# A hybrid decoder layer on one core: x and two of its input blocks first, memory keys and values after the S5 branch

## The chip, the cores and the metric

The kernel runs on one core of one Trainium2 chip. The metric is the device time of one execution in microseconds (us), the median of several runs; a profile of one further execution shows where its time goes.

## The reference, cut to what matters

One step of one layer, for a prompt of 512 tokens and 8 single sample tokens that share the weights (520 columns in all):

```python
h = rmsnorm(x, norm1_g)
u, q, k, v, qm, gl = split(h @ w_in)          # 512 | 768 | 768 | 768 | 512 | 3 x 1024 columns
A = glu(gelu(S5(u)))                          # 32 groups, 64 complex states each, scan over tokens
B = dilated_window_attention(q, k, v) @ w_att_o
C = cross_attention(qm, rmsnorm(mem, mem_norm_g) @ w_mem_kv) @ w_mem_o   # 256 memory tokens; samples: cached k, v
x = x + (sum_b sigmoid(gl_b) * branch_b) @ w_out
a, v2 = split(rmsnorm(x, norm2_g) @ w_up)
x = x + (gelu(causal_conv3(a)) * v2) @ w_down
y = rmsnorm(x, final_norm_g)
```

D_MODEL is 1024, D_FF 2816. The states, keys, values and memory keys and values are outputs too.

## The kernel before, in words

**Products.** Activations lie with features on the 128 partitions, in eight blocks of 520 columns. Every fp32 product is three products of high and low parts: the weight tile (128x1024, 512 KB) is fetched by `wload` (L160, on the SP queue), rounded to its high part by ScalarE (L163, `wh`), and VectorE takes the rest (L80, `wl`). One call of `dense` makes one block of 128 output features: for each of eight k blocks, in two halves of 260 columns, wh by xh (L192), wh by xl (L193) and wl by xh (L195), 48 matmuls in all. L80 is the line of the helper `tt`, so all tensor-by-tensor work of VectorE and GpSimd bears it. There are two PSUM tiles for dense blocks, two buffers for raw weights and four for high and low parts; `wahead(AHEAD)` keeps four tiles on their way.

**Order.** A framework sets the order of each engine's queue from the program order, priorities (`urgent`) and its own cost estimates; each engine then runs its queue strictly in that order and waits on semaphores. On top of it a class `Side` runs generators beside the dense blocks: after every k block `side.pe(...)` advances a clock by the block's cost, and a generator whose time has come may issue its next piece, so that small matmuls of S5, attention and samples stand between dense ones.

**Stages.** The stages stand in this order: memory statistics and keys (`ps_mk`, L494 to L498), memory values (`ps_mv`, L519 to L521), and the four S5 input blocks u0 to u3; memory queries qm0 to qm3, k0 to k5 and q0 to q5 with S5 beside them; v0 to v5 with memory attention (`mem_prompt`) beside them; `ssm_gated(0)` to `(5)` (a gate block `ps_g` and the GLU pair `ps_ga`, `ps_gb`: 96 matmuls each) with windowed attention (`att_prompt`) beside them; then `ssm_gated(6)`, `(7)` and eight early gate blocks with the samples (`att_sample`, `mem_sample`) beside them; then the branch outputs (`ps_at`, `ps_me`), w_out, w_up and w_down. These last four, from the branch outputs on, take more time than all the rest together and are untouched.

**S5.** `s5_params` turns the parameters into powers (pwr, pwi, rwr, rwi) and bbr, bbi by about 150 small VectorE operations; `s5_rot` builds tables of rotations rc, rsn (shared between GpSimd and VectorE); `s5_tables(fb)` makes gr, gi, e1, e2 of block fb (VectorE, with the products t0 to t3 on GpSimd), which PE transposes (`ps_gt`, L616) and multiplies (`ps_k`, L625); `s5_batches` multiplies by the inputs (`ps_v`, L655), goes through a chain on VectorE and GpSimd (products tx, sums wr and wi, two scans, products ty, results fr and fi) and then needs fr and fi on PE again (`ps_y`, L703 and L709). `s5_z` brings gelu(y) back through memory as the tiles zz.

**Samples.** `mem_sample` takes the cached memory keys in four chunks of 1 MB (mkc, two buffers; `ps_sms`, L1139), a softmax, a transpose (`ps_smt`, L1161), the products mzz on VectorE, and the cached values in four chunks of 1 MB (mvc, the same two buffers; `ps_smo`, L1175). Chunk c+2 is issued by L1179 and can only start when the matmuls of chunk c have ended. Then msso, `ps_smot` and omem lead to oh, ol, which `ps_me` needs.

```python
        po = ps_small("ps_smo")
        for c in range(4):
            ...
            if c < 2:
                vn = q.tile([P, 2, 2, 512], F32, tag=f"mkc{c % 2}", name=f"mvc{c + 2}")
                S.dma_start(vn, I["smv"][c + 2])
                vcs.append(vn)
            yield 1, 2.5
```

Of the kernel before, what the change touches and what calls it, by code (L numbers as in the profile page):

```python
# [60 lines left out]
def build(nc, tc, I, O):  # L61
# [53 lines left out]
    def weights():  # L115
        for f in range(4):
            yield f"mk{f}", I["wmk"][f]
        for c in range(4):
            yield f"mv{c}", I["wmv"][c]
        for i in [IN0[n] + f for n, f in FIRST] + list(range(20, 26)):  # L120
            yield f"in{i}", I["wi"][i]
# [165 lines left out]
    m_cm, mp = pool("memkv", 1, side="right")  # L287
    qm = mp.tile([P, 4, SEQ], F32, name="qm")
    mkT = mp.tile([P, 4, NMEM], F32, name="mkT")
    mv = mp.tile([P, 2, 512], F32, name="mv")  # L290
    ms_cm, ms = pool("memstage", 1, side="right")
    memT = ms.tile([P, KB, NMEM], F32, name="memT")
    memh = ms.tile([P, KB, NMEM], F32R, name="memh")
    meml = ms.tile([P, KB, NMEM], F32R, name="meml")
# [1275 lines left out]
```

## Time and profile before

| | |
|---|---|
| median of 3 runs | 990.66 us (988.93 to 990.77) |
| the profiled execution, its own time | 990.76 us |
| its span in the trace | 989.0 us |
| PE (TensorE) busy | 947.1 us, 96% |
| DVE (VectorE) busy | 554.0 us, 56% |
| ACT (ScalarE) busy | 299.6 us, 30% |
| POOL (GpSimd) busy | 192.6 us, 19% |
| granted TensorE clock, mean | 0.98 |

1.76 us of the profiled execution lie outside of its span. Times in the trace count from the span's start. The busy time of PE is the union of its matmuls, whether they run at the full or at half the clock: a stretch at half clock looks busy and does half the work. A row's "[3.58 <-DVE gr L80]" says that the engine stood idle for 3.58 us and that the work that ended this was VectorE's on gr.

### The profile page before, as it was taken

How to read it: one execution, taken by the hardware profiler on the slowest of the kernel's cores; microseconds unless marked ns; L12 is line 12 of the kernel's file. 1: busy time of each engine (PE TensorE's matmuls, PEld its weight loads, DVE VectorE, ACT ScalarE, POOL GpSimd, SP SyncE). 2: the span in 40 equal slices, each digit the busy share in tenths (PEclk: the TensorE clock that was granted, in tenths of full speed). 3: DMA queues.
4: the chain of work that ended last, by engine and by line, in shares of the span. 5: the costliest groups of instructions: out<-in, count | busy, mean ns of one | idle time of the engine just before them, and what ended most of it. 6: DMA issues, size and time to landing. Idle time of an engine off the chain costs nothing.

```text
span 989.0 us, 19819 instructions
## 1 busy us (share of the span) xinstructions
PE 947.1 (96%) x8373; PEld 914.1 (92%) x8373; DVE 554.0 (56%) x1017; ACT 299.6 (30%) x480; POOL 192.6 (19%) x261
## 2 busy tenths in 40 slices
PE   8798899989999999999999999999999999999996
PEld 7597899877999998999999999999999999999995
DVE  6999976445455434344655676555555555423234
ACT  6412232224354322123323233322323322222220
POOL 4359542012003301100210350000000000012110
PEclk9998999989999999999999999999999999999998
DMA  7543335531322127563322532223223223332312
GB/s 236 188 152 107 92 104 192 149 95 65 133 87 75 44 68 243 195 229 116 96 91 92 162 118 95 86 93 100 86 86 106 88 85 97 91 99 80 97 39 87
DMA packets 47305, 112.36 MB, mean 114 GB/s; under 512 B 13600, under 2 KB 21408, under 8 KB 45600
## 3 DMA queue, kind: packets, MB, share of 16 engines
q1 hardware_dynamic: 47216, 111.09, 35.0%
q8 instruction: 66, 1.08, 0.4%
q14 instruction: 23, 0.19, 0.1%
HBM read 101.36 MB, written 9.71 MB: 112 GB/s over the span
## 4 chain that ended last, share of the span: by engine, by line
PE 58%; DVE 1%; POOL 1%; ACT 0%; issue 0%; DVEq 0%; ACTq 0%; POOLq 0%
PE ps_y L192 4%; PE ps_y L195 4%; PE ps_y L193 4%; PE ps_uv L195 4%; PE ps_uv L192 4%; PE ps_uv L193 4%; PE ps_ua L192 4%; PE ps_ua L195 4%; PE ps_ua L193 4%; PE ps_g L192 3%; PE ps_g L195 3%; PE ps_g L193 3%; PE ps_x L195 2%; PE ps_x L192 2%; PE ps_x L193 2%; PE ps_me L193 1%
## 5 line engine op out<-in xcount | busy, mean ns | idle before, releaser
L192 PE MATMUL ps_g<-xh,wh_in 128*128 128x260 f32 x384 | 102.0, 287 | 0.0
L193 PE MATMUL ps_g<-xl,wh_in 128*128 128x260 f32 x384 | 99.9, 282 | 0.0
L192 PE MATMUL ps_y<-gh,wh_dn 128*128 128x260 f32 x352 | 93.0, 283 | 0.0
L193 PE MATMUL ps_y<-gl,wh_dn 128*128 128x260 f32 x352 | 93.0, 283 | 0.0
L192 PE MATMUL ps_uv<-hh,wh_uv 128*128 128x260 f32 x352 | 91.9, 282 | 0.0
L192 PE MATMUL ps_ua<-hh,wh_ua 128*128 128x260 f32 x352 | 91.8, 282 | 0.0
L193 PE MATMUL ps_uv<-hl,wh_uv 128*128 128x260 f32 x352 | 91.6, 282 | 0.0
L193 PE MATMUL ps_ua<-hl,wh_ua 128*128 128x260 f32 x352 | 91.6, 282 | 0.0
L163 ACT CAST wh_in<-wr_in 128x1024 fp32r<-128x1024 f32 x50 | 52.3, 1051 | 106.4 <-PE ps_g L193 35.8
L195 PE MATMUL ps_g<-xh,wl_in 128*128 128x260 f32 x384 | 77.2, 283 | 0.0
L192 PEld LDWEIGHTS ps_g<-xh,wh_in 128*128 128x128 f32 x384 | 72.3, 188 | 2.6 <-issue 2.4
L195 PE MATMUL ps_y<-gh,wl_dn 128*128 128x260 f32 x352 | 74.4, 282 | 0.0
L80 DVE TENSOR_TENSOR wl_in<-wr_in,wh_in 128x1024 fp32r<-128x1024 f32 x49 | 67.5, 1378 | 8.8 <-ACT wh_in L163 7.2
L193 PEld LDWEIGHTS ps_g<-xl,wh_in 128*128 128x128 f32 x384 | 72.2, 188 | 0.0
L195 PE MATMUL ps_uv<-hh,wl_uv 128*128 128x260 f32 x352 | 71.2, 283 | 0.0
L195 PE MATMUL ps_ua<-hh,wl_ua 128*128 128x260 f32 x352 | 70.9, 283 | 0.0
L192 PEld LDWEIGHTS ps_uv<-hh,wh_uv 128*128 128x128 f32 x352 | 66.4, 189 | 0.0
L192 PEld LDWEIGHTS ps_ua<-hh,wh_ua 128*128 128x128 f32 x352 | 66.3, 188 | 0.0
L193 PEld LDWEIGHTS ps_y<-gl,wh_dn 128*128 128x128 f32 x352 | 66.2, 188 | 0.0
L192 PEld LDWEIGHTS ps_y<-gh,wh_dn 128*128 128x128 f32 x352 | 66.2, 188 | 0.0
L193 PEld LDWEIGHTS ps_uv<-hl,wh_uv 128*128 128x128 f32 x352 | 66.1, 188 | 0.0
L193 PEld LDWEIGHTS ps_ua<-hl,wh_ua 128*128 128x128 f32 x352 | 66.1, 188 | 0.0
(440 smaller groups left out, 2497.5 us busy)
## 6 DMA issues: line engine op xcount, KB each, us to landing
wr_in<-in_wi SPq DMA_DIRECT2D x50, 512.0 KB, 3.4
wr_ua<-in_wup SPq DMA_DIRECT2D x22, 512.0 KB, 3.3
wr_uv<-in_wup SPq DMA_DIRECT2D x22, 512.0 KB, 3.3
wr_dn<-in_wdn SPq DMA_DIRECT2D x16, 448.0 KB, 3.3
wr_glu<-in_wglu SPq DMA_DIRECT2D x8, 512.0 KB, 3.2
mkc<-in_smk SPq DMA_DIRECT2D x4, 1024.0 KB, 6.4
mvc<-in_smv SPq DMA_DIRECT2D x4, 1024.0 KB, 6.2
wr_out<-in_wout SPq DMA_DIRECT2D x8, 512.0 KB, 3.2
```

Of the source, the lines that this page charges most:

```text
L80: e.tensor_tensor(o, a, b, op)
L163: A.copy(hi[:, a:b], raw[:, a:b])
L192: T.matmul(ps[:, a:b], lhsT=wh, rhs=ah[:, t0:t1], start=st, stop=False)
L193: T.matmul(ps[:, a:b], lhsT=wh, rhs=al[:, t0:t1], start=False, stop=False)
L195: T.matmul(ps[:, a:b], lhsT=wl, rhs=ah[:, t0:t1], start=False, stop=en)
```

## The change

**Start.** x comes first, k block by k block (`x_part`), with the first two weight tiles in halves (`wload_begin`); u0 and u1 are computed together as the k blocks arrive. The squares of x are kept in the unused tiles of q, k and v and summed by PE (`square_sums`: 16 matmuls of 128x32 by 260 columns) instead of by GpSimd's additions. u0 and u1 are copied out raw by ScalarE and scaled later. From here to the end of u3 VectorE and ScalarE run in program order (`manual_schedule`), and the operations of `s5_params` are collected in a list and issued a few at a time (`params(n)`).

**Middle.** k, q and v come next with S5 beside them. `s5_rot` is on GpSimd alone, the products tx and ty are on VectorE alone, and the stages of S5 are pipelined: `s5_state` of a block is issued before `s5_out` of the block before, with two buffers for fr, fi and ug.

**After S5.** The memory is loaded and normalised, then qm0 to qm3, memory keys and memory values are computed; memory attention runs beside `ssm_gated(0)` and on, windowed attention beside the following ones up to the eighth, and the samples beside the eight early gate blocks alone.

The core of the diff (left out: moved lines, allocations, the evacuation of u, memory keys, whose code is as before):

```diff
-FIRST = order("u0", "u1", "u2", "u3", "qm0", "qm1", "qm2", "qm3", "k0", "k1", "k2", "k3", "k4", "k5",
-              "q0", "q1", "q2", "q3", "q4", "q5")
+FIRST = order("u0", "u1", "u2", "u3", "k0", "k1", "k2", "k3", "k4", "k5", "q0", "q1", "q2", "q3", "q4", "q5",
+              "v0", "v1", "v2", "v3", "v4", "v5", "qm0", "qm1", "qm2", "qm3",
+              "mk0", "mk1", "mk2", "mk3", "mv0", "mv1", "mv2", "mv3")
...
+    def wload_begin(name, src):
+        raw = wp.tile([P, 1024], F32, tag="wr", name=f"wr_{name}", bufs=WB[0])
+        hi = wp.tile([P, 1024], F32R, tag="wh", name=f"wh_{name}", bufs=WB[1])
+        lo = wp.tile([P, 1024], F32R, tag="wl", name=f"wl_{name}", bufs=WB[1])
+        wfly.append((name, hi, lo))
+
+        def part(a, b):
+            S.dma_start(raw[:, a:b], src[:, a:b])
+            A.copy(hi[:, a:b], raw[:, a:b])
+            tt(V, lo[:, a:b], raw[:, a:b], f32(hi[:, a:b]), OP.subtract)
+        return part
...
+    pending = []
+
+    class Later:
+
+        def __init__(self, engine):
+            self.engine = engine
+
+        def __getattr__(self, op):
+            return lambda *a: pending.append((getattr(self.engine, op), a))
+
+    def params(n):
+        for _ in range(min(n, len(pending))):
+            f, a = pending.pop(0)
+            f(*a)
...
+    def square_sums(ps, sqs, n, first, last):
+        for j, sq in enumerate(sqs):
+            for p, t0, t1 in ps:
+                T.matmul(p[32 * j:32 * j + 32, 0:t1 - t0], lhsT=ones[:, 0:32], rhs=sq[:, t0:t1], start=first,
+                         stop=last, skip_group_check=True)
...
+    in_order = tc.manual_schedule(engines={mybir.EngineType.DVE, mybir.EngineType.Activation})
+    in_order.__enter__()
+    s5_params()
+    w0, w1 = (wload_begin(*next(wsrc)) for _ in range(2))
+    xsq = []
+    w0(0, 512)
+    params(5)
+    x_part(0)
+    w1(0, 512)
+    params(3)
+    for k in (1, 2, 3):
+        x_part(k)
+        xsq.append(x_square(k - 1))
+        params(3)
+    w0(512, 1024)
+    params(3)
+    w1(512, 1024)
+    params(3)
+    for k in (4, 5, 6, 7):
+        x_part(k)
+        xsq.append(x_square(k - 1))
+        params(4)
+    xsq.append(x_square(KB - 1))
...
+    ps01 = [ps_dense(f"ps_u{f}") for f in range(2)]
+    w01 = [wget(f"in{f}") for f in range(2)]
+    for k in range(KB):
+        for f in range(2):
+            dense(ps01[f], w01[f], k, xacts[k:k + 1], first=(k == 0), last=(k == KB - 1))
+    for n in (1, 2):
+        wahead(n)
+        params(12)
+    raw01 = []
+    for f in range(2):
+        r = spare[1][:, (3 + f) * NT:(4 + f) * NT]
+        A.copy(r, ps01[f][:, ALL])
+        raw01.append(r)
+
+    psq = [ps_small(f"ps_xq{h}") for h in range(2)]
+    w = wget("in2")
+    u2 = ps_dense("ps_u2")
+    dense(u2, w, 0, xacts[:2], last=False)
+    for i in (0, 4):
+        square_sums([(psq[h], *HALVES[h][2:]) for h in range(2)], xsq[i:i + 4], NT, i == 0, i == 4)
+    for h in range(2):
+        A.copy(xacc[:, HN * h:HN * h + HN], psq[h][:, 0:HN])
+    dense(u2, w, 2, xacts[2:], first=False)
+    wahead(2)
+    params(10)
+    xrt = rms_stat(ps_small("ps_xr"), [xacc], NT, "xr", stp, 32)
+    w = wget("in3")
+    u3 = ps_dense("ps_u3")
+    dense(u3, w, 0, xacts[:4], last=False)
+    rms_bcast([ps_small("ps_xb0"), ps_small("ps_xb1")], xrt, NT, rstd, "xr", stp)
+    dense(u3, w, 4, xacts[4:], first=False)
+    evac_u(2, u2[:, PR], u2[:, SM])
+    for f in range(2):
+        evac_u(f, raw01[f][:, 0:SEQ], raw01[f][:, SEQ:NT])
+    evac_u(3, u3[:, PR], u3[:, SM])
+    wahead(3)
+    params(20)
+    wahead(AHEAD)
+    params(1000)
+    in_order.__exit__(None, None, None)
...
-    pmk = []
-    for f in range(4):
...
+    def mem_v(c):
+        if not pmv:
+            pmv.extend(ps_small(f"ps_mv{b}") for b in range(2))
...
                 tt(G, a, lr, br, OP.mult)
                 tt(G, b, li, bi, OP.mult)
                 tt(G, rc[:, g0:g1, m:2 * m], a, b, OP.subtract)
-                tt(V, c, lr, bi, OP.mult)
-                tt(V, d, li, br, OP.mult)
-                tt(V, rsn[:, g0:g1, m:2 * m], c, d, OP.add)
+                tt(G, c, lr, bi, OP.mult)
+                tt(G, d, li, br, OP.mult)
+                tt(G, rsn[:, g0:g1, m:2 * m], c, d, OP.add)
...
-            if fb == 0:
-                s5_rot()
-                s5_decay()
-            yield 0, TD0 if fb == 0 else TD1
+            yield 0, TD1
...
+            state = fb, ug, *s5_state(fb, ug)
+            yield 1, 0
+            if sent is not None:
+                yield from s5_out(*sent)
+            sent = state
+        yield 0, BD0
+        yield from s5_out(*sent)
...
+        tt(V, tx[0], v0, c_, OP.mult)
+        tt(V, tx[1], v1, s_, OP.mult)
+        tt(V, tx[2], v1, c_, OP.mult)
+        tt(V, tx[3], v0, s_, OP.mult)
+        tt(V, wr, tx[0], tx[1], OP.add)
+        tt(V, wi, tx[2], tx[3], OP.subtract)
...
+        tt(V, ty[0], sr_, c_, OP.mult)
+        tt(V, ty[1], si_, s_, OP.mult)
+        tt(V, ty[2], sr_, s_, OP.mult)
+        tt(V, ty[3], si_, c_, OP.mult)
+        tt(V, fr[:, :, 9:73], ty[0], ty[1], OP.subtract)
+        tt(V, fi[:, :, 9:73], ty[2], ty[3], OP.add)
...
+    for n, f in FIRST[4:22]:
+        ps = dense_in(IN0[n] + f, f"{n}{f}")
+        if n == "v":
+            vT = vtp.tile([P, SEQ], F32, tag="vT", name=f"vT{f}")
+            evac_qk(vT, vs[:, f % 2, f // 2], ps, f >= 2)
+            S.dma_start(O["vT"][:, f], vT)
+            vtasks.append(side.add(vtrans(f, vT), 3))
         else:
-            evac_qk(qT[:, f], qs[:, f], ps, f >= 2)
+            evac_qk((kT if n == "k" else qT)[:, f], (ks if n == "k" else qs)[:, f], ps, f >= 2)
...
+    for f in range(4):
+        ps = dense_in(IN0["qm"] + f, f"qm{f}")
+        evac_qk(qm[:, f], qms[:, f], ps, False)
+        if f == 1:
+            pmq = ps_small("ps_mq")
+            for i in (0, 4):
+                square_sums([(pmq, 0, NMEM)], msq[i:i + 4], NMEM, i == 0, i == 4)
+            A.copy(macc, pmq[:, 0:NMEM])
+        elif f == 2:
+            mrt = rms_stat(ps_small("ps_mr"), [macc], NMEM, "mr", ms, 32)
+    for f in range(4):
+        if f == 0:
+            rms_bcast([ps_small("ps_mb")], mrt, NMEM, mrs, "mr", ms)
+        mem_k(f)
+    for c in range(4):
+        mem_v(c)
...
+    nd = 0
+    mtasks = [side.add(mem_prompt(j), 8 * j) for j in range(4)]
+    while running(mtasks):
+        ssm_gated(nd)
+        nd += 1
+    close(ma_cm)
+    close(m_cm)
...
-    for d in range(6):
-        ssm_gated(d)
+    while running(atasks) and nd < KB:
+        ssm_gated(nd)
+        nd += 1
...
-    for d in (6, 7):
+    for d in range(nd, KB):
         ssm_gated(d)
```

**PE around q5.** ps_y10 and ps_y11 are the outputs of S5 block 1, wh_in19 and wl_in19 the weight of q5. Before, q5 stands right behind q4; the last rows of q4 and the first of q5:

```order
L192 MATMUL ps_q4_2553<-xh_97,wh_in18_2218 128x260
L193 MATMUL ps_q4_2553<-xl_98,wh_in18_2218 128x260
L195 MATMUL ps_q4_2553<-xh_97,wl_in18_2219 128x260 x2
L192 MATMUL ps_q5_2610<-xh_97,wh_in19_2335 128x260
L193 MATMUL ps_q5_2610<-xl_98,wh_in19_2335 128x260
```

After, ps_v of block 2 (16 matmuls) and ps_y of block 1 (48 matmuls) stand between q4 and q5; the end of the latter and the first rows of q5 on PE:

```order
L817 MATMUL ps_y11_1623<-fi_1_1249,e2_1_957 64x72
L197 MATMUL ps_q5_2087<-xh_100,wh_in19_1738 128x260
L198 MATMUL ps_q5_2087<-xl_101,wh_in19_1738 128x260
L197 MATMUL ps_q5_2087<-xh_100,wh_in19_1738 128x260
L198 MATMUL ps_q5_2087<-xl_101,wh_in19_1738 128x260
L200 MATMUL ps_q5_2087<-xh_100,wl_in19_1739 128x260 x2
```

The fifth matmul of q5 is the first that needs wl_in19.

**VectorE around wl_in19.** qT are the evacuations of q blocks, tx to fi the chain of an S5 block. Before, wl_in19 stands three q blocks ahead of its use:

```order
L80 TENSOR_TENSOR wl_in18_2219<-wr_in18_2217,wh_in18_2218 128x1024
L682 MEMSET fr_3_2475 128x4
L683 MEMSET fi_3_2476 128x4
L80 TENSOR_TENSOR wl_in19_2336<-wr_in19_2334,wh_in19_2335 128x1024
L80 TENSOR_TENSOR qT_80<-ps_q2_2342,rstd_76 128x128x4
```

After, it stands behind the evacuation of q4 and the whole chain of block 2, of which these are the last rows:

```order
L783 SCALAR_TENSOR_TENSOR s3_2_1598<-rh_2_1594,wi_2_1587 128x256
L80 TENSOR_TENSOR tywr_2_1609<-s2_2_1597,rsn_114 128x256
L80 TENSOR_TENSOR tytx0_2_1607<-s2_2_1597,rc_113 128x256
L80 TENSOR_TENSOR tytx1_2_1608<-s3_2_1598,rsn_114 128x256
L80 TENSOR_TENSOR tywi_2_1610<-s3_2_1598,rc_113 128x256
L80 TENSOR_TENSOR fr_2_1601<-tytx0_2_1607,tytx1_2_1608 128x4x64
L80 TENSOR_TENSOR fi_2_1602<-tywr_2_1609,tywi_2_1610 128x4x64
L80 TENSOR_TENSOR e1_3_1704<-cri_122,pwr_115 128x576
L80 TENSOR_TENSOR wl_in19_1739<-wr_in19_1737,wh_in19_1738 128x1024
```

The chain's first row waits for ps_v of block 2, which PE runs behind q4. The low part of v1, wl_in21, stands in the same way behind the chain of block 3.

**PE at the end of the samples.** Before, the four chunks of ps_smo have 24 gate matmuls (ps_g) between them, and 36 ahead of the first; two neighbouring rows at the second chunk's start:

```order
L195 MATMUL ps_g30_5294<-xh_97,wl_in53_5054 128x260 x2
L1175 MATMUL ps_smo_5247<-mvc1_5146,mzz_5197 32x128 x16
L192 MATMUL ps_g30_5294<-xh_97,wh_in53_5053 128x260
L193 MATMUL ps_g30_5294<-xl_98,wh_in53_5053 128x260
L192 MATMUL ps_g30_5294<-xh_97,wh_in53_5053 128x260
```

After, the gates have run out by then:

```order
L1270 MATMUL ps_smt_5424<-ident_75,msp_5378 128x128 x2
L197 MATMUL ps_g23_5367<-xh_100,wh_in45_5144 128x260
L198 MATMUL ps_g23_5367<-xl_101,wh_in45_5144 128x260
L197 MATMUL ps_g23_5367<-xh_100,wh_in45_5144 128x260
L198 MATMUL ps_g23_5367<-xl_101,wh_in45_5144 128x260
L200 MATMUL ps_g23_5367<-xh_100,wl_in45_5145 128x260 x2
L1284 MATMUL ps_smo_5446<-mvc0_5374,mzz_5427 32x128 x16
L1284 MATMUL ps_smo_5446<-mvc1_5376,mzz_5427 32x128 x16
L1284 MATMUL ps_smo_5446<-mvc2_5463,mzz_5427 32x128 x16
L1284 MATMUL ps_smo_5446<-mvc3_5481,mzz_5427 32x128 x16
L1295 MATMUL ps_smot_5517<-ident_75,msso_5515 128x128
L197 MATMUL ps_at0_5545<-ah_5529,wh_am0_5203 128x260
```

Six gate matmuls are left between ps_smt and ps_smo, and none between the chunks.

## Rows read from the trace of the kernel before

**Rows 1.** Windows by stage: length, busy us (instructions) of PE, PEld, DVE, ACT, POOL; clock; DMA

```profile
0.00:13.40 13.40, 10.29 (x43) 9.40 (x44) 6.90 (x19) 7.87 (x18) 4.08 (x10) 1.00 0.73 223
13.40:46.60 33.20, 24.87 (x142) 20.80 (x142) 30.69 (x84) 18.21 (x27) 15.32 (x12) 0.95 0.57 192
46.60:73.00 26.40, 24.52 (x203) 24.10 (x201) 24.39 (x96) 7.35 (x8) 12.96 (x16) 1.00 0.55 182
73.00:171.00 98.00, 90.20 (x988) 85.06 (x992) 81.45 (x131) 24.86 (x48) 52.69 (x57) 0.95 0.41 124
171.00:208.00 37.00, 35.39 (x383) 33.39 (x372) 17.79 (x34) 9.85 (x20) 5.92 (x10) 0.95 0.38 108
208.00:274.60 66.60, 61.24 (x468) 53.49 (x467) 30.48 (x56) 21.65 (x54) 9.82 (x18) 0.92 0.34 114
384.00:464.00 80.00, 77.56 (x874) 71.65 (x874) 32.23 (x55) 20.31 (x31) 8.33 (x10) 0.98 0.54 187
```

**Rows 2.** Waits of PE, whole span: for whom, us in total, times, longest

```profile
PE ps_mv L520 <- DVE wl_mv L80: 7.4, 3, 4.0
PE ps_y L709 <- DVE fr L80: 4.9, 2, 3.3
PE ps_gt L616 <- DVE gr L80: 3.6, 1, 3.6
```

**Rows 3.** Windows again: five stretches at half clock before 274.6 us

```profile
79.00:85.00 6.00, 5.49 (x24) 5.09 (x25) 6.00 (x8) 0.00 (x0) 6.00 (x6) 0.50 0.01 1
119.00:122.60 3.60, 3.60 (x20) 3.60 (x19) 2.19 (x2) 2.09 (x2) 0.00 (x0) 0.53 0.75 180
177.20:180.70 3.50, 3.50 (x36) 2.98 (x35) 2.78 (x5) 1.26 (x3) 0.00 (x0) 0.51 0.37 70
211.40:218.20 6.80, 6.00 (x91) 4.79 (x92) 3.41 (x7) 2.05 (x5) 0.00 (x0) 0.50 0.52 157
235.30:238.70 3.40, 3.40 (x16) 3.07 (x14) 0.78 (x2) 0.59 (x1) 1.85 (x4) 0.50 0.39 145
```

**Rows 4.** Timeline of DVE: evacuations of two consecutive undisturbed q blocks

```profile
194.30 1.09 DVE L80 TENSOR_TENSOR qT<-ps_q,rstd 128x512 f32<-128x512 f32 x1 [3.53 <-PE ps_q L195]
...
200.06 1.09 DVE L80 TENSOR_TENSOR qT<-ps_q,rstd 128x512 f32<-128x512 f32 x1 [4.66 <-PE ps_q L195]
```

**Rows 5.** Timeline of PE: samples' score chunk; transpose; first value chunk

```profile
414.28 1.07 PE L1139 MATMUL ps_sms<-mkc,mqz 128*32 128x256 f32 x16
...
434.15 0.38 PE L1161 MATMUL ps_smt<-ident,msp 128*128 128x128 f32 x2
438.77 1.08 PE L1175 MATMUL ps_smo<-mvc,mzz 128*32 128x128 f32 x32
```

**Rows 6.** Groups of DVE by form, 75 to 220 us: busy, mean ns, idle before

```profile
L80 DVE TENSOR_TENSOR wl_in<-wr_in,wh_in 128x1024 fp32r<-128x1024 f32 x17 | 24.1, 1418 | 3.3 <-ACT wh_in L163 3.1
...
L80 DVE TENSOR_TENSOR zz<-zt,zz 128x512 fp32r<-128x512 f32 x3 | 3.4, 1145 | 1.2 <-ACT zz L730 1.2
L80 DVE TENSOR_TENSOR tx<-vi,rsn 128x256 f32<-128x256 f32 x4 | 3.4, 839 | 0.0
...
L80 DVE TENSOR_TENSOR e<-cri,pwi 128x576 f32<-128x576 f32 x4 | 3.0, 753 | 0.0
...
L677 DVE TENSOR_TENSOR_SCAN s<-rh,wr 128x256 f32<-128x256 f32 x4 | 2.7, 663 | 0.0
...
L80 DVE TENSOR_TENSOR fi<-tywr,tywi 128x256 f32<-128x256 f32 x4 | 1.7, 414 | 0.0
```

**Rows 7.** Timeline of DVE: the samples' products mzz

```profile
434.57 2.35 DVE L80 TENSOR_TENSOR mzz<-ps_smt,mqmask 128x1024 f32<-128x1024 f32 x2 [3.07 <-PE ps_smt L1161]
```

**Rows 8.** Tile mvc: its DMAs

```profile
DMA to landing us min/median/max: 5.1/6.2/7.5
```

**Rows 9.** Groups of DVE by form, 0 to 75 us: tiny operations in two places

```profile
L80 DVE TENSOR_TENSOR mr_rq<-mr_ri 128x2 f32<-128x2 f32 x3 | 2.7, 887 | 0.0
...
L80 DVE TENSOR_TENSOR xr_rq<-xr_ri 128x5 f32<-128x5 f32 x3 | 0.5, 157 | 0.0
```

More of the change, by code (lines that the diff above doesn't have):

```diff
@@ L115, in weights @@
     def weights():
-        for f in range(4):
[L117 to L121, printed above, removed]
+        for n, f in FIRST:
+            yield (f"{n}{f}", I["wm" + n[1]][f]) if n in ("mk", "mv") else (f"in{IN0[n] + f}", I["wi"][IN0[n] + f])
         def ssm(d):
@@ L286, in build @@
     kT = qkp.tile([P, 6, SEQ], F32, name="kT")
[L287 to L294, printed above, removed]
+    v_cm, vp = pool("v", 1, side="right")
+    vtok = vp.tile([P, 4, 768], F32, name="vtok")
+    st_cm, stp = pool("start", 1, side="right")
+    uts = [stp.tile([P, 8, 80], F32, name=f"ut{f}") for f in range(4)]
+    for t in uts:
+        G.memset(t, 0.0)
     h_cm, hp = pool("h")
@@ new lines, in s5_out @@
+    def s5_out(fb, ug, fr, fi):
+        e1, e2, gt, tm = tabs[fb]
+        zg = bt([P, 8, 72], "zg", fb)
+        py = [ps_small(f"ps_y{fb}{h}") for h in range(2)]
+        for lp in range(4):
+            cols = slice(lp * 72, (lp + 1) * 72)
+            for h in range(2):
+                g = 2 * lp + h
+                for m in range(0, P, 64):
+                    T.matmul(py[h][m:m + 64, cols], lhsT=tm[:, g, m:m + 64], rhs=ug[:, g, 0:72],
+                             start=True, stop=False, skip_group_check=True)
+            for e, f, last in ((e1, fr, False), (e2, fi, True)):
+                for m in range(0, P, 64):
+                    for h in range(2):
+                        rows = slice(64 * h, 64 * h + 64)
+                        T.matmul(py[h][m:m + 64, cols], lhsT=e[rows, lp, 1:9].rearrange(fl)[:, m:m + 64],
+                                 rhs=f[rows, lp, 0:72], start=False, stop=last, skip_group_check=True)
+            if lp < 3:
+                yield 0.7, BD1
+        for h in range(2):
+            A.activation(zg.rearrange("p (l h) x -> p h l x", h=2)[:, h],
+                         py[h][:, :288].rearrange("p (l x) -> p l x", l=4), AF.Gelu_apprx_tanh)
+        s5done["bat"] = fb + 1
+        s5t.append(side.add(s5_z(fb, zg), 5))
+        yield 0.7, 0
@@ new lines, in build, with vtrans @@
+    zh, zl = zz[:, 0:4], zz[:, 4:8]
+    s5_rot()
+    s5_decay()
+    b5_cm, b5 = pool("s5b")
+    s5t.append(side.add(s5_tables(0)))
+    s5t.append(side.add(s5_tables(1), TD4))
+    s5t.append(side.add(s5_batches()))
+    def vtrans(f, vT):
+        pt = ps_small(f"ps_vt{f}")
+        for b in range(4):
+            T.transpose(pt[:, b * P:(b + 1) * P], vT[:, b * P:(b + 1) * P], ident)
+        A.copy(vtok[:, :, f * P:(f + 1) * P], pt.rearrange("p (b x) -> p b x", b=4))
+        yield 0.5, 0
```

394 lines of the change are left out of this document (157 added, 237 removed).

## The prediction, written before the changed kernel was run

> **What bounds the kernel now.** I read the busy shares first: PE 96% of the span, so only work added to PE, time in which PE stands, and half clock can move the end. Then the windows by stage [rows 1]. They show where PE stands: 3.11 us idle to 13.4 us, 8.33 us more to 46.6, then 1.88, 7.80, 1.61 and 5.36 in the stages up to 274.6 us, where the first gate block begins. From there to the end hardly anything is lost, and the samples' stage loses only 2.44 of its 80 us. In the first 73 us VectorE is busy in 6.90 of 13.40, 30.69 of 33.20 and 24.39 of 26.40 us: it paces the start. Next the waits of PE [rows 2]: memory values for wl_mv 7.4, ps_y for fr 4.9, ps_gt for gr 3.6, all of them on VectorE. Last the clock [rows 3]: five stretches of 23.3 us in sum at 0.50 to 0.53, that is at 1.2 GHz, each behind a gap or a thin stretch of PE. Half of 23.3 is 11.6 us lost while PE looks busy.
>
> The loss before, in one number. Undisturbed q blocks follow each other in 200.06 - 194.30 = 5.76 us [rows 4], so a dense block costs 5.75 us, 0.12 us a matmul. Scaling the other matmuls by their columns, I count as PE work up to 274.6 us: 26 dense blocks 149.5, memory keys 11.4 and values 11.1, S5 four times 6.2, norms 2, memory attention 15.3, transposes of v and rest 3.3, in all 217.3 (an estimate, good to some 3 us). So 274.6 - 217.3 = **57.3 us** are lost there: about 23 before u0, 1 to 2 beside u0 to u3, 33 after. Idle time (7.8 + 1.6 + 5.4) and half clock (11.6) explain 26.4 of the 33; the rest, 6.6, are gaps too small to list. All this work stays in the changed kernel, only elsewhere, so the change is worth: added work, plus its own losses, less 57.3.
>
> **The change, part by part.**
>
> *Work added to PE.* 16 matmuls of 128x32 sum the squares of x, 8 those of the memory. The samples' scores are the same form: 8 of 256 columns take 1.07 us [rows 5] (the trace counts each twice). So 2.1 + 1.1 = 3.2 us. Above, if neighbours on the same 32 columns do not overlap as the scores' do: four passes of 0.11 us each for 16, 6.9 + 1.1 = 8.0. I take **4.1**, near the row of the same form.
>
> *Start, up to k0.* Eight k blocks of x (266 KB each) and two weight tiles are 3.2 MB; at the 223 GB/s of the first 13.4 us [rows 1] they land at 14 to 16 us, so u0 and u1 (11.5 us of PE) end at about 18.5: 7 lost, with the cold clock. Then PE has u2, the squares, u3 and the norm; k0 waits for u2's tile, which needs the normaliser: 3. Together **10** (9 to 12), for 23 + 1.5 before. The memory's wait for wl_mv goes; it is late nowhere else.
>
> *Tables of S5 blocks 0 and 1.* Between the normaliser and the first finished gr VectorE has some 85 operations: four evacuations of u (1.4 each), nine low parts (1.2 to 1.4), powers, bbr, bbi, and the first gr, gi. End to end this is 32 to 37 us, so gr_0 is there at 68 to 73 us when PE gets to it at 70; gr_1, 7 to 9 us later, meets 8 us of PE work. I take 3 to 5 of waiting with one half-clock stretch: **7** (2 to 10). Nothing else hides it; PE's queue stands.
>
> *Block 2's tables* within q2: **2.5** (1 to 4), by the 3.6 of gr before.
>
> *q5 behind the chain of block 2.* wl_in19 now stands behind the chain. From the end of ps_v on PE: 0.8 for ScalarE's vr and vi, 12 operations of 256 columns at 0.33 to 0.41 where GpSimd is quiet (fi 414 ns), two scans (663), zz (1145), e1_3 (753), wl_in19 (1.2): 9.4 to 10.4 us [rows 6]. With the prices beside GpSimd (tx 839, wl_in 1418) it is 13. PE has ps_y of block 1 (3.2) and four matmuls of q5 (0.5) meanwhile. So it stands 5.7 to 9, and comes back at half clock, which cost 1.7 to 3.4 a time [rows 3]. **8.5** (4 to 12). Before, the same low part stood three blocks ahead and cost nothing.
>
> *v1 behind the chain of block 3.* The same without e1_3, with one evacuation of v: **7.5** (4 to 11).
>
> *Memory stage:* weights at one tile per 2.85 us of PE, **1** (0 to 2). *Memory attention* beside gates instead of v: **4** (2 to 6). *Small gaps* as before, some less: **4** (2 to 7).
>
> *Samples.* Before, 576 gate and GLU matmuls lie beside them, now 384, and behind ps_smt only 6 (0.7 us). mzz takes 2.35 us [rows 7], which leaves 2 idle; ps_smo came 4.6 us behind ps_smt before [rows 5], all covered. Then chunks 0 and 1 (1.08 each). Chunk 2 is issued when chunk 0 has ended, and lands 6.2 us later (5.1 to 7.5) [rows 8]: 5.1 idle behind chunk 1. Chunk 3 follows a transfer that runs beside it: 1. Then msso, omem, the splits: 2. Idle 10, and half clock behind it, 2: **12** (9 to 14). Before, 24 matmuls (2.9 us) and a chunk stood between chunks, and it cost nothing.
>
> *ScalarE, GpSimd, SP.* s5_rot on GpSimd is some 50 operations of 0.3 to 1 us, up to 33 us from about 29 us on. rc and rsn are first needed by tx of block 0, about 80 us: hidden; without that cover the overrun would be PE's. SP's queue: the weight of q5 stands behind block 2's copies dk and zt, whose landing I count in the chain.
>
> **Sum:** 10 + 7 + 2.5 + 8.5 + 7.5 + 1 + 4 + 4 + 12 = 56.5 lost; 4.1 + 56.5 - 57.3 = **+3.3 us**. The profiled execution took 990.76, 0.10 above the median, so I forecast **994.1 us**. The start's gain (some 14) is eaten by q5, v1 and the samples (28).
>
> **Where trace and skill differ.** Two-operand VectorE operations of a few elements take 0.16 us where GpSimd is idle (xr_rq, 157 ns), and 0.89 beside GpSimd's sums of squares (mr_rq, 887 ns) [rows 9]; wl_in goes only from 1.2 to 1.42 [rows 6]. The Trainium skill (SBUF — State Buffer, SBUF: two separate sides) says that a VectorE operation with two SBUF inputs and a GpSimd operation that reads SBUF exclude each other for a whole instruction. By that rule the added GpSimd work would hold up the parameters one operation at a time and the sum would be that of rival 2; the tiny operations agree with it, the long ones hardly show it.
>
> **Rivals.**
>
> 1. *VectorE keeps pace; faster.* tx and ty no longer meet GpSimd's, so the chains run at the short prices and zz is not late. Then the losses are: start 9, tables 3 and 1.5, q5 5.5, v1 5, memory 0 and 2.5, gaps 3, samples 11, in sum 40.5; work 3.2; 3.2 + 40.5 - 57.3 = -13.6: **977 us**. For it: fi's 414 ns, and 23 us lost before u0, which surely go. Against: VectorE is full to 110 us, and the two chains cannot be shorter than the 3.7 us of PE work.
>
> 2. *GpSimd's rotations hold up VectorE; slower.* From 36 to about 60 us some 55 tiny operations stand beside s5_rot. If a third to a half of them wait 0.4 to 0.7 us, gr_0 comes 8 to 12 us later and PE, with nothing behind it, stands: tables 7 becomes 16: 994 + 9 = **1003 us**. It decides once gr_0 is later than some 74 us: every further microsecond is then PE's. For it mr_rq, against it the long operations.
>
> 3. *The waits only change places; no change.* If the half-clock stretches behind q5 and v1 fall away (3 to 4 us), 994 becomes **990.5**: what the start frees is paid back behind it.
>
> **How the numbers follow.** The forecast's own case 0.36 (range 991 to 1000), rival 1 0.35, rival 2 0.14, rival 3 0.15. 0.2% is 2 us, about what a measurement of this kernel can tell from no change. Faster by more (under 988.7): 0.36, nearly all of it rival 1. Within: 0.16, rival 3 and the edge of the forecast. Slower: 0.48. The sum of all low ends is 3.2 + 33 - 57.3 (970), that of all high ends over 1010; both need every term on one side. I give **973 to 1006**: a tenth left out at either end, with rival 1 to 4 us below its sum and rival 2 to 3 above.
>
> **What would show it.** In the changed profile: k0 at 37 to 40 us; a wait of ps_gt for gr of 2 to 5; one wait of ps_q for wl_in of 5 to 9 and one of ps_v of 4 to 8, both with the clock at 0.5 behind them; in the samples' stage waits of ps_smo for mvc of 5 to 7 in sum and for mzz of 2. The forecast is wrong if ps_q and ps_v wait under 3 us each (rival 1), if gr waits over 10 (rival 2), or if k0 starts later than 44 us.

## The result and the profile after

The changed kernel takes **1002.25 us** (median of 4 runs, 1001.34 to 1004.22), the kernel before, run beside it, 990.37 (4 runs, 988.93 to 990.77): ratio **1.0125**, interval 1.0106 to 1.0144. It is slower by 11.9 us where 3.3 were forecast. The profiled execution took 1002.75 us with a span of 1000.6. Sign and range held, but 1002.25 lies outside the 991 to 1000 of the forecast's own case and next to the 1003 of the second rival: the range held because it reached out to that rival.

First the windows by stage of the changed kernel, as in [rows 1]: length, then busy us (instructions) of PE, PEld, DVE, ACT and POOL; granted clock, DMA share, GB/s.

```profile
0.00:13.40 13.40, 10.18 (x48) 8.73 (x49) 6.83 (x26) 8.71 (x15) 3.01 (x10) 0.87 0.78 267
13.40:39.40 26.00, 25.38 (x219) 23.34 (x217) 22.59 (x84) 11.44 (x17) 8.88 (x33) 1.00 0.36 119
39.40:70.00 30.60, 30.01 (x245) 29.58 (x246) 29.09 (x76) 5.25 (x5) 15.44 (x21) 1.00 0.50 147
70.00:96.00 26.00, 15.75 (x191) 13.29 (x191) 25.71 (x37) 6.26 (x17) 21.23 (x18) 0.80 0.29 83
96.00:136.00 40.00, 38.39 (x487) 36.15 (x487) 27.13 (x55) 8.72 (x21) 7.99 (x10) 1.00 0.47 129
136.00:152.00 16.00, 9.81 (x96) 8.62 (x94) 12.39 (x22) 5.02 (x12) 3.34 (x2) 0.68 0.13 40
152.00:172.00 20.00, 16.10 (x210) 14.97 (x209) 11.01 (x24) 5.30 (x12) 0.89 (x2) 0.84 0.53 141
172.00:205.50 33.50, 32.94 (x342) 32.00 (x342) 13.48 (x18) 11.80 (x17) 0.00 (x0) 0.99 0.56 172
205.50:257.90 52.40, 49.92 (x367) 46.66 (x366) 26.15 (x48) 19.74 (x31) 0.00 (x0) 0.97 0.45 152
257.90:412.00 154.10, 151.36 (x1309) 140.82 (x1307) 75.34 (x192) 61.91 (x151) 24.84 (x49) 1.00 0.31 104
412.00:457.00 45.00, 43.31 (x511) 39.03 (x512) 15.22 (x32) 9.72 (x15) 7.11 (x10) 1.00 0.56 201
457.00:475.00 18.00, 9.70 (x148) 7.24 (x147) 6.35 (x10) 4.16 (x8) 0.00 (x0) 0.75 0.39 153
```

A stretch's visible loss is its length less PE's busy time times the clock. Up to 70 us it is 4.5 + 0.6 + 0.6 = 5.7, where [rows 1] give 14.6 for the first 73: the start gained 8.9. Three stretches stand out behind it: the tables of S5 blocks 0 and 1 (70 to 96 us, 26 - 15.75 x 0.80 = **13.4**), q5 (136 to 152, **9.3**) and v1 (152 to 172, **6.5**). Up to the first gate block, at 257.9 us, the visible loss is 41.4, against 40.5 up to 274.6 in [rows 1]: what the start gained is lost again. Then comes the tail of the samples (457 to 475), **10.7**; the whole samples' stage of before lost 4.0 (80 - 77.56 x 0.98).

The waits of PE in the changed kernel (in us: total, times, longest), as in [rows 2]:

```profile
PE ps_gt L710 <- DVE gr L80: 10.8, 3, 7.4
PE ps_smo L1284 <- DMA mvc<-in_smv: 5.6, 2, 5.1
PE ps_q L200 <- DVE wl_in L80: 4.0, 1, 4.0
...
PE ps_vt L875 <- DVE vs L80: 2.5, 1, 2.5
PE ps_q L197 <- ACT wh_in L168: 2.2, 1, 2.2
PE ps_v L197 <- ACT wh_in L168: 2.1, 1, 2.1
PE ps_v L200 <- DVE wl_in L80: 1.8, 1, 1.8
...
PE ps_smo L1284 <- DVE mzz L80: 1.3, 2, 0.7
```

The waits for wl_mv and fr of before are gone, and gr went from 3.6 to 10.8. q5 waits twice for its weight, for the high part (wh_in) and then for the low part (wl_in), together 6.2; v1 waits 3.9 in the same two steps. The samples wait 5.6 for mvc and 1.3 for mzz.

Why gr_0 is late, in the timeline of VectorE (start, duration, operation, idle before in brackets):

```profile
46.40 0.58 DVE L347 TENSOR_TENSOR s5t<-rwr 128x16 f32<-128x16 f32 x1
46.91 0.16 DVE L347 TENSOR_TENSOR s5t<-rwi 128x16 f32<-128x16 f32 x1
47.11 0.60 DVE L347 TENSOR_TENSOR rwr<-s5t,s5t 128x16 f32<-128x16 f32 x1
...
71.55 0.69 DVE L80 TENSOR_TENSOR gr<-bbr,rwr 128x512 f32<-128x512 f32 x1
72.16 1.59 DVE L80 TENSOR_TENSOR gi<-bbr,rwi 128x512 f32<-128x512 f32 x1
73.68 1.65 DVE L80 TENSOR_TENSOR e<-cri,pwr 128x576 f32<-128x576 f32 x1
75.25 1.76 DVE L80 TENSOR_TENSOR e<-cri,pwi 128x576 f32<-128x576 f32 x1
76.93 1.03 DVE L80 TENSOR_TENSOR kT<-ps_k,rstd 128x512 f32<-128x512 f32 x1
...
77.88 0.76 DVE L80 TENSOR_TENSOR gr<-gr,t 128x512 f32<-128x512 f32 x1
```

and of GpSimd in the same two places:

```profile
45.36 1.59 POOL L80 TENSOR_TENSOR vtok<-rc,rotc 128x256 f32<-128x256 f32 x1
46.92 0.75 POOL L80 TENSOR_TENSOR rsn<-vtok 128x256 f32<-128x256 f32 x1
47.74 0.65 POOL L80 TENSOR_TENSOR vtok<-rsn,rots 128x256 f32<-128x256 f32 x1
...
71.68 1.52 POOL L80 TENSOR_TENSOR t<-bbi,rwi 128x512 f32<-128x512 f32 x1 [3.17 <-DVE bbi L347]
73.17 1.54 POOL L80 TENSOR_TENSOR t<-bbi,rwr 128x512 f32<-128x512 f32 x1
```

Beside the rotations (vtok, rsn, rc) the tiny operations take 0.48 to 0.68 us, with one of 0.16 here and there. Beside GpSimd's products t the 512-wide gi takes 1.59 where gr, begun just ahead of them, took 0.69, and the e products take 1.65 and 1.76 where e of that shape took 753 ns on average before [rows 6]. What these rows lengthen by is what is left of the neighbour's operation: t begins at 71.68 and ends at 73.20, and gi ends 0.55 us after it. The subtraction that ends gr_0 starts at 77.88, behind both products and an evacuation of k, and the transposes of ps_gt start at 78.69.

For q5, ScalarE's timeline of the changed kernel:

```profile
133.57 0.40 ACT L765 COPY vr<-ps_v 128x288 f32<-128x288 f32 x1 [13.85 <-PE ps_v L760]
...
137.06 0.71 ACT L822 ACTIVATE zg<-ps_y 128x288 f32<-128x288 f32 x2
...
137.76 1.06 ACT L168 CAST wh_in<-wr_in 128x1024 fp32r<-128x1024 f32 x1
```

VectorE's low part of the same weight,

```profile
142.84 1.22 DVE L80 TENSOR_TENSOR wl_in<-wr_in,wh_in 128x1024 fp32r<-128x1024 f32 x1
```

and the DMA issues of SP, which put the weights behind S5's copies, with the times to landing of the two weights among them (least, median, most):

```profile
115.69 0.40 SPq L743 DMA_DIRECT2D ug<-du  x1
119.97 0.58 SPq L729 DMA_DIRECT2D dk<-kt  x1
120.64 0.80 SPq L832 DMA_DIRECT2D zt<-dz  x1
121.49 1.86 SPq L729 DMA_DIRECT2D dk<-kt  x3
123.39 1.06 SPq L166 DMA_DIRECT2D wr_in<-in_wi  x2
...
DMA to landing us min/median/max: 4.7/5.4/6.1
```

No weight is issued in these rows before 123.39: S5's kt is not there yet, and the weight stands behind it in one queue. But the transfer is not the last thing that q5 waits for. Both weights have landed by some 130 us, while ScalarE stands idle for 13.85 us up to 133.57; the cast to wh_in follows only at 137.76, because it stands behind vr, vi, zz and zg of the S5 blocks in ScalarE's order, and the low part at 142.84, behind block 2's chain in VectorE's. A cast (1.06) and a low part (1.22) right behind the landing would have ended by 133 (an estimate), ahead of 136.7, where PE first stood for this weight. v1 is the same: its weight, issued at 155.57, has landed by 161, and PE first stands for it at 164.1, but the cast comes at 165.07, behind zz and zg.

### The profile page after: what moved, and what is told of

It is laid out like the page before. It is cut to its first block, busy times and chain, and to the rows that moved or that the text cites. A ratio compares the mean times of both kernels' runs of the same rounds, so it can differ in the third digit from the quotient of the medians.

```text
span 1000.6 us, 19893 instructions
## 1 busy us (share of the span) xinstructions
PE 947.6 (95%) x8421; PEld 913.9 (91%) x8421; DVE 547.3 (55%) x1015; ACT 302.6 (30%) x486; POOL 160.0 (16%) x251
## 3 DMA queue, kind: packets, MB, share of 16 engines
q8 instruction: 66, 1.08, 0.5%
## 4 chain that ended last, share of the span: by engine, by line
PE 55%; DVE 2%; DMA 1%; POOL 0%; ACT 0%; issue 0%; DVEq 0%; ACTq 0%
PE ps_y L197 4%; PE ps_y L200 4%; PE ps_uv L200 4%; PE ps_y L198 4%; PE ps_uv L197 4%; PE ps_uv L198 4%; PE ps_ua L197 4%; PE ps_ua L200 4%; PE ps_ua L198 4%; PE ps_g L197 3%; PE ps_g L200 3%; PE ps_g L198 3%; PE ps_x L200 2%; PE ps_x L197 2%; PE ps_x L198 2%; DMA mvc<-in_smv 1%
## 5 line engine op out<-in xcount | busy, mean ns | idle before, releaser
L80 DVE TENSOR_TENSOR wl_in<-wr_in,wh_in 128x1024 fp32r<-128x1024 f32 (+1 forms) x52 | 65.8, 1268 | 20.4 <-ACT wh_in L168 13.3
```

Of the source, the lines that this page charges most:

```text
L80: e.tensor_tensor(o, a, b, op)
```

## The experiments

Ratios are to the kernel before on the same chip; the changed kernel's is 1.0125. The medians in us are given beside them; between batches only the ratios compare.

**1. Own tiles for the samples' values.**

```
-        for c in range(2):
-            vc = ... tag=f"mkc{c % 2}", name=f"mvc{c}")
+        for c in range(4):
+            vc = ... tag=(f"mkc{c}" if c < 2 else f"mvc{c}"), name=f"mvc{c}")
```

(the loads of chunks 2 and 3 inside the loop fall away)

> Chunks 2 and 3 of the cached memory values get tiles of their own, so that their transfers need not wait for ps_smo of chunks 0 and 1. Theory (the samples' tail is 12 us of the loss, about half of it this wait): the waits of ps_smo for mvc go from 5.6 us to under 0.5, the half clock behind them shrinks, the time falls by 5.5 to 8 us, to 994 to 997. Rival (the tail is bound by mzz, msso and omem on VectorE, or the transfers only land later): the time falls by 0 to 2 us.

995.87 us, ratio 1.0073 (1.0055 to 1.0091), so 0.0052, or 5.1 us, less. The wait for mvc is gone, those for mzz (1.3) stay. What is queued behind a buffer is about half of the samples' loss.

**2. Without the rotations on GpSimd.**

```
-    s5_rot()
+    G.memset(rc, 0.5)
+    G.memset(rsn, 0.5)
```

> s5_rot's products on GpSimd are left out and rc, rsn are filled with a constant (the S5 output and the prompt's states are then not the reference's). Theory (GpSimd's rotations hold up VectorE's parameter operations between 38 and 55 us): the 16-column operations there take 0.16 us instead of about 0.55, gr of block 0 is ready some 6 us earlier, PE's first wait of ps_gt falls from 7.4 to 1 to 2 us, the half clock behind it goes, and the time falls by 7 to 10 us, to 992 to 995. Rival (VectorE's list between the normaliser and gr is too long by itself): the first wait stays at 6 to 7.4 us and the time within 2 us of 1002.

1000.02 us, ratio 1.0114 (1.0081 to 1.0147). The runs spread over 6.7 us, so the time alone decides nothing. The trace shows more: a row of VectorE's tiny operations,

```profile
42.56 0.17 DVE L347 TENSOR_TENSOR s5t<-rwr 128x16 f32<-128x16 f32 x1
```

and the first transpose of PE,

```profile
72.61 1.11 PE L710 MATMUL ps_gt<-ident,gr 128*128 128x128 f32 x4 [4.51 <-DVE gr L80]
```

The operation that took 0.58 takes 0.17, and so do its neighbours; the first transpose comes 6.1 us earlier (78.69 to 72.61), and a wait of 4.5 remains, where the theory had 1 to 2. Not all of the 6.1 belongs to the rotations: k0 starts at 37.44 here and at 39.44 in the changed kernel, and in the profiles of experiments 3 to 5, which keep the rotations and the start, at 37.4 to 37.5. Counted from VectorE's first copy of rstd (the normaliser's result) to the last operation on gr of block 0 it is 36.4 us here, 40.5 in the changed kernel and 41.1 to 41.5 in experiments 1 and 3 to 5: the rotations lengthen this list by 4 to 5 us. gi and e stay at 1.6 to 1.8 beside t, since the t are still there. The 7 to 10 us that the theory expected in the time did not come; 0.0011 less than the change is within the noise.

**3. S5's copies on GpSimd's queue.**

```
-                S.dma_start(dkv[q], kt[32 * q:32 * q + 16])
+                G.dma_start(dkv[q], kt[32 * q:32 * q + 16])
```

(so too for tm, ug, dz and zt)

> The transfers of S5 (dk, tm, ug, dz, zt) are issued by GpSimd's queue instead of SP's; nothing else is changed, but the framework then puts wl_in19 and wl_in21 ahead of the chains of blocks 2 and 3 on VectorE. Theory (the weights of q5 and v1 are late because their transfers stand in SP's queue behind S5's, and their splits therefore behind the chains): the waits of ps_q and ps_v for wh_in and wl_in, 10.1 us in sum, fall under 2, with the half clock behind them; the time falls by 9 to 13 us, to 989 to 993. Rival (the wait only moves: fi comes later by the two splits, or GpSimd's queue, which now waits for kt and zg, hands t0 to t3 over late): ps_y or ps_gt wait 5 us or more in their place, and the time stays within 3 us of 1002.

989.35 us, ratio 1.0007 (0.9989 to 1.0025): almost the whole 1.0125, some 11.7 us, from five kinds of DMA on another queue. Of SP's issues,

```profile
99.13 33.05 SPq L166 DMA_DIRECT2D wr_in<-in_wi  x6
```

and the first waits of PE in the view of this run:

```profile
PE ps_gt L710 <- DVE gr L80: 13.5, 3, 7.6
PE ps_smo L1284 <- DMA mvc<-in_smv: 8.0, 2, 7.5
```

SP now issues six weights from 99.13 us on, where before there was none from 96 to 123. No wait for wl_in or wh_in of q and v is left, and the memory queries start at 193.17 instead of 205.46, 12.3 us earlier. The orders of ScalarE and VectorE moved with it: the cast of q5's weight, which stood behind zg, now stands ahead of block 2's chain (107.13 instead of 137.76), and so does its low part (110.81 instead of 142.84). The wait for gr is not smaller, that for mvc is larger. So the loss at q5 and v1 comes from the place of the weights, but this run changes two things, the queue and, through the framework, the orders behind it. The rows of the changed kernel, where the weight lay ready for 7 us or more before its cast, speak for the orders; a run with the old queue and the new orders was not made.

**4. Half of tx and ty back on GpSimd.**

```
-        tt(V, tx[0], v0, c_, OP.mult)
+        tt(G, tx[0], v0, c_, OP.mult)
```

(so too for tx[2], ty[0] and ty[2])

> The products tx0, tx2, ty0 and ty2 go back to GpSimd, as in the kernel before (one part undone). Theory (beside GpSimd the chain is longer, so the low parts behind it come later): the waits of ps_q and ps_v for their weights grow from 10.1 us in sum to 13 to 17, the time rises by 3 to 7 us, to 1005 to 1009. Rival (VectorE is the bound and every operation taken from it helps): the chain is no longer than before, the waits fall by 1 to 3 us and the time is 999 to 1002.

1006.14 us, ratio 1.0178 (1.0161 to 1.0195): 5 us slower, as the theory had it, but not by the waits that it named: ps_v waits 6.2 for wh_in (2.1 in the changed kernel) and ps_q 4.0 (2.2), and neither waits for wl_in any more, so the sum is 10.2 as before (10.1), not 13 to 17. What grew are the waits for gr, 14.9 instead of 10.8, with one of 3.6 behind q5's. The cast of q5's weight comes at 139.94, 2.2 later, behind a longer chain, though its transfer was issued at 123.43 as before: that again speaks for ScalarE's order. This part of the change is worth keeping.

**5. Samples with cover.** Four tiles shared by keys and values, all loads early, and the score chunks yield less of the gates' work:

```
-            yield 1, 2.5
+            yield 1, 0.5
...
+        for c in range(4):
+            vc = ... tag=f"mkc{c}", name=f"mvc{c}")
```

> Four tiles for the cached memory keys, which the memory values reuse (so no transfer waits for the chunk two before it), and 0.5 instead of 2.5 us of dense work between the score chunks: 36 gate matmuls stand ahead of the first value chunk and 24 and 18 between the next, as in the kernel before. Theory (the samples' tail costs 12 us because gate matmuls that cover it have run out, of which the waits for mvc are half): PE waits for neither mvc nor mzz, and the time falls by 9 to 12 us against the changed kernel, to 990 to 993, 4 to 6 us below the run in which only the value chunks have tiles of their own (995.9). Rival (the tail's other half is msso, omem and the splits on VectorE and ScalarE, which stay uncovered): within 2 us of that run.

994.75 us, ratio 1.0055 (1.0033 to 1.0077), 0.0070 less than the change. From the first ps_smt to the projection the window of the profiled run reads:

```profile
445.60:461.20 15.60, 14.37 (x211) 13.10 (x209) 6.74 (x9) 4.33 (x7) 0.00 (x0) 1.00 0.50 184
```

1.2 us lost at full clock, where the changed kernel lost 10.7; the samples' projection ps_x starts 12.7 us earlier in the profile, and PE waits for neither mvc nor mzz. But the profiled execution took 989.99 us, one of the fastest of ten that spread over 8.7, and the median is only 7 us below the change. Against experiment 1 (1.0073) that is 0.0018, with intervals that overlap: by the time the rival, within 2 us of that run, is not excluded, and what the cover adds to own tiles is shown in the trace alone. Why the runs vary stays open.

**6. gr first.** The subtractions for gr and gi are written ahead of the products e1 and e2.

```
-            tt(V, e1, cr, wr, OP.mult)
-            tt(V, e2, cr, wi, OP.mult)
...
+            tt(V, e1, cr, wr, OP.mult)
+            tt(V, e2, cr, wi, OP.mult)
```

> In s5_tables the subtractions that finish gr and gi stand ahead of the products e1 and e2 again, as before (one part undone). Theory (gr of block 0 is late because on VectorE's list e1, e2, each 1.7 us beside GpSimd, and the evacuation of k4 stand ahead of its last operation): gr_0 is ready 3 to 5 us earlier, PE's first wait of ps_gt falls from 7.4 to 2 to 4.5 us, the time by 2 to 5 us. Rival (GpSimd's t0 is what ends last, or e1, e2, gr_1 only come later by as much): the first wait falls by less than 1.5 us or the others grow by as much, and the time stays within 1.5 us of 1002.

1000.18 us, ratio 1.0109 (1.0085 to 1.0132). The first ps_gt starts at 75.80 instead of 78.69 and waits 5.7, not 7.4; in sum the waits for gr are 10.9, and ps_k waits 1.1 for e. From the copy of rstd to the last operation on gr of block 0 it is 35.5 us, 5 to 6 less than the 40.5 to 41.5 named in experiment 2. Only some 1.6 us come out in the time, which the intervals do not tell from none: block 0 is served, and what stood ahead of gr is late elsewhere. The theory's 2 to 4.5 for the first wait was missed, and the rival's growth of the other waits came.

**7. Without the hand-set order.**

```
-    in_order = tc.manual_schedule(engines={... DVE, ... Activation})
+    in_order = contextlib.nullcontext()
```

> The hand-set order of VectorE and ScalarE is taken away; the framework orders them (everything else as in the changed kernel). gr of block 0 then stands behind the evacuation of k1 instead of k4. Theory (the hand-set list, which spreads the parameters between evacuations of k blocks, is what makes gr_0 late): the wait of ps_gt for gr falls from 7.4 to under 2 us and the half clock behind it goes; k0 starts within 2 us of 39.4; the time falls by 5 to 10 us. Rival (the order is what lets u0, u1 and the normaliser keep pace with x): k0 starts 3 to 8 us later and the time is 1000 to 1008.

989.71 us, ratio 0.9999 (0.9986 to 1.0012), 12.5 us less, more than the theory's 5 to 10. k0 starts 4.6 us *later* (44.05), as the rival had it, ps_xb waits 3.4 for the normaliser, and yet the first ps_gt starts 13.1 us earlier (65.61), with a wait of 4.9 for gr; ps_q and ps_v wait for no weight. The hand-set order buys the start and pays for it with the tables and the weights. SP still waits 18.8 us for kt (25.0 in the changed kernel), and the weights of q5 and v0 still stand behind dk in its queue (issued at 113.64). But block 2's chain now runs beside q3 and q4, and PE reaches q5 only at 144.70, 12 us after its low part has ended (132.53). So a late transfer by itself does not make PE wait.

**8. Three edits together** (3, 5 and 6).

> S5's transfers on GpSimd's queue, the samples covered as in the run above, and gr, gi ahead of e1, e2, together. If the three losses are separate, the changes add up: 11.7 + 9 to 12 + 2 to 5 off 1002, so 974 to 980 us, below the kernel before by 1 to 1.5%. If they share a cause (one stall that only moves), the sum is under 15 us and the time 985 or more.

981.47 us, ratio 0.9917 (0.9886 to 0.9948). The parts took off 0.0118, 0.0070 and 0.0016, in sum 0.0204; together they take off 0.0208. That fits separate losses, and without them the change is faster than the kernel before. The forecast of 974 to 980 was missed by 1.5 us, because the samples and gr had brought less by themselves than it took for them.

**9. Hand-set order for the start alone.** It ends behind the evacuation of u.

```
+    in_order.__exit__(None, None, None)
```

> The hand-set order ends with the evacuations of u; what is left of the parameters, and the tables, the framework orders (gr of block 0 behind the evacuation of k1, as without hand-set order). Theory (the order is good for the start, where it lets k0 begin at 37 to 39 us instead of 44, and bad for the parameters behind it): k0 at 37 to 40 us, first ps_gt at 62 to 68 us, and 4 to 7 us below the run without hand-set order (989.7), so 982 to 986. Rival (the parameters set the end of this stretch, and an earlier k0 only waits longer for gr): the first wait of ps_gt grows by what k0 gains, and the time is 988 to 991.

994.05 us, ratio 1.0039 (1.0015 to 1.0063). The hoped-for early k0 did not come: it starts at 44.79, ps_xb waits 3.9 for xr_dg. My guess is that the loosened part behind moves work ahead of the normaliser. The first ps_gt starts at 70.43. Theory and rival both missed that, and the time; whether the early start can be had without the order behind it stays open.

**10. Edits 3, 5, 6 and 9 together.**

> The three mended losses (S5's transfers on GpSimd's queue, the samples covered, gr and gi first) and the hand-set order up to the evacuations of u alone. If the gains stay separate: 981.5 of the three, less 4 to 8 us, so 973 to 978 us. If the hand-set order's loss was the same wait of q5 and v1 that the queue has already mended: 980 to 983.

981.55 us, ratio 0.9914 (0.9890 to 0.9938), the same as experiment 8, as the second forecast had it: k0 at 44.59, the first ps_gt at 64.86 instead of 73.36, which pays for the later start.

**11. The kernel before with edit 3.**

```
-        S.dma_start(zt, dz.rearrange("i p x -> p i x"))
+        G.dma_start(zt, dz.rearrange("i p x -> p i x"))
```

> The kernel before, with S5's transfers on GpSimd's queue. Theory (the queue hurts only where weights stand behind S5's transfers and their splits behind a chain, which the change brought): within 2 us of the kernel before, 987 to 991. Rival (SP's queue holds up weights in the kernel before as well): 3 us or more below it.

994.2 us, ratio 1.0039 (1.0023 to 1.0055): 3.9 us *slower*, which neither theory nor rival had. ps_mt waits 3.9 for pm on GpSimd, ps_y 5.7 for fr (4.9 before). The queue is not better as such; it helps only with the orders that the framework makes for the changed kernel.

**12. Edits 3, 5 and 6, and no hand-set order.**

> The kernel with the three edits (S5's DMAs on GpSimd's queue, the samples' chunks in four tiles, gr ahead of the products), and the hand-set order switched off as well. Taken alone, the queue was worth 13 us and the order switched off 12.5, and both removed the waits of ps_q and ps_v. Theory, the two are one loss reached from two sides: what is left over for the order is the tables of block 0 (first ps_gt at 73.4 with the three edits, at 65.6 without hand order), some 4 to 7 us of them, and the normaliser's wait (3.4) is given back: 975 to 981, ratio 0.985 to 0.991. Rival, separate losses: 981.5 - 12 = 969, ratio 0.98. Second rival, the tables are late in another place once the samples and the queue are mended: 981 to 985, ratio 0.991 to 0.996, a wait of ps_gt for gr over 8 in sum and the samples' ps_x later than 532.

**978.38 us**, ratio **0.9878** (0.9857 to 0.9899), within what the theory gave. The waits of PE that remain ahead of the samples' end:

```profile
PE ps_gt L710 <- DVE gi L80: 4.4, 1, 4.4
PE ps_xb L250 <- DVE xr_dg L247: 3.6, 3, 1.7
PE ps_gt L710 <- issue: 2.8, 1, 2.8
PE ps_q L197 <- DVE qs L80: 2.5, 1, 2.5
```

Alone the order was worth 0.0126, on top of the three edits 0.0039, with intervals that overlap: so most of its price is something that the three edits mend as well, by the waits of q5 and v1 the weights' place. This is the lowest ratio here, 1.2% ahead of the kernel before, though not told apart from experiments 8 and 10.

## Why the prediction was right in its sign and too low

The yardstick is the prediction's own: work up to the first gate block, less what the change moves behind it. 217.3 less 15.3 of memory attention plus 4.1 added is 206.1 us; the gate starts at 257.9, so **51.8** are lost where 40.5 were forecast (start 10, tables 7, block 2 and gaps 6.5, q5 8.5, v1 7.5, memory 1). Term by term:

- **Start, 10 forecast.** k0 began at 39.44, in the forecast's 37 to 40. Less 23 for u, 2.1 for the squares and 2 for the norm, 12.3 were lost. Right in mechanism, 2 short, just outside its 9 to 12.
- **Tables of blocks 0 and 1, 7 (2 to 10) forecast: the step that failed.** 13.4 were lost. gr_0 was forecast at 68 to 73 us, and its last operation began at 77.88. What was mis-sized is VectorE's list from the normaliser to gr_0, 32 to 37 us in the forecast: it took 40.5. The rotations cost 4 to 5 of that (experiment 2); the price of their neighbours in the sum was that of an idle GpSimd, although [rows 9] held the other price (its 887 ns is the mean of one operation of 148 and two of some 1257). A second part, 5 to 6, was not in the forecast at all: the e products at 1.6 to 1.8 us beside t and an evacuation of k, standing in the written order ahead of gr's end (experiment 6). What the two are worth in time is not shown, since the medians of experiments 2 and 6 do not differ from the change by more than the noise.

The prediction held that long operations "hardly show" the exclusion. They do: 0.69 against 1.59 and 0.75 against 1.76. It named its own test, that gr waits over 10: 10.8. So rival 2's sign came, on top of the forecast's other terms; its mechanism, the rotations, is about half of the lateness, and it had been given 0.14. The Trainium skill (SBUF — State Buffer, SBUF: two separate sides) says that a VectorE operation with two SBUF inputs and a GpSimd operation that reads SBUF exclude each other for a whole instruction; these rows agree for the tiny operations and for gi and e. The low parts, which the prediction took for an exception, fit as well:

```profile
44.84 1.64 DVE L80 TENSOR_TENSOR wl_in<-wr_in,wh_in 128x1024 fp32r<-128x1024 f32 x1
```

```profile
43.80 1.60 POOL L80 TENSOR_TENSOR vtok<-rsn,rotc 128x256 f32<-128x256 f32 x1
```

The rotation that was running ends at 45.40, and wl_in (1.2 alone) ends 1.08 after it, at 46.48. The next rotation, begun at 45.36, takes 1.59 instead of the 0.61 of the same form at 50.23 and ends 0.47 after wl_in. So wl_in paid only the rest of a short neighbour, and GpSimd paid the remainder.

- **q5, 8.5 (4 to 12) forecast, 9.3 lost; v1, 7.5 (4 to 11), 6.5 lost.** Right, with half clock behind it (0.68 and 0.84 in the windows). But the wait fell on two things, wh_in on ScalarE first and wl_in after, where the prediction named wl_in alone for both. The prediction did see the weight behind dk and zt in SP's queue, and left it in the chain's price. Its mechanism, the low part behind the chain in VectorE's order, stands: the weight had landed 7 us or more before its cast. Experiment 3 removes the loss by another queue and the other orders that came with it, and does not tell the two apart.
- **Memory stage, 1 forecast, 4.0 lost** (52.4 - 49.92 x 0.97). The weights are not what it was lost on: 2.5 of it is the wait of ps_vt for vs, shown above, in front of a transpose at 209.06. No run studies it.
- **Block 2 and small gaps, 6.5 forecast.** 51.8 less the terms above (45.5) leaves 6.3. This is a remainder, with the 3 us of doubt in 217.3 in it; the windows show 3.1 lost in these stretches (39.4 to 70, 96 to 136 and 172 to 205.5).
- **Samples 12, memory attention 4.** Behind the gate's start the changed profile takes 1002.75 - 257.86 - 15.3 = 729.6 us, the one before 990.76 - 274.59 = 716.2: 13.4 more, for 16 forecast. The tail has 10.7 of it, and experiment 1 shows one half in the time, chunk 2 behind chunk 0's buffer; the other, too little work beside the value chunks, shows in the trace of experiment 5 only. Memory attention lost less than its 4, at most the 2.7 visible in the stretch of 257.9 to 412.

The sum is 4.1 + 51.8 + 13.4 - 57.3 = 12.0, against 3.3 forecast: 11.3 too little up to the gate, 2.6 too much behind it. The measured 11.9 is 12.0 by construction of the yardstick and is no second proof; the experiments are.

The sign came out by the terms for q5, v1 and the samples, which were nearly met; that the range held is owed to its reaching over rival 2 as well. Rival 1 (VectorE keeps pace) fell with the waits for q5, rival 3 with the half clock, which came back at both places.

## What to carry to other kernels

When a start is made earlier, ask for each table behind it what stands beside it on the other vector engine, and price it by the row that has the same neighbour, not by the cleanest one. A weight that stood behind copies of computed data in one queue was issued 24 us later here than with those copies in another queue (123.39 against 99.13), but what made PE wait was the place of its cast and its split behind a chain: follow issue, landing, cast and split one by one, and see which comes last. Covering work moved away from the tail of a double buffer is a cost of the change even where the buffer's code is not touched.
